# First layer's MLP in phases, with seven block products for most of its first matrix

## The chip, the core and the metric

The kernel runs on one core of a Trainium2 chip. The metric is device time in microseconds. Five engines work side by side, each through its own queue in order: TensorE (PE, matmuls, with its weight loads as PEld), VectorE (DVE), ScalarE (ACT), GpSimd (POOL) and SyncE (SP), whose queue issues nearly all the transfers.

## What is computed

A two-layer decoder trunk over 1024 tokens of width 1024. Layer 0 mixes by an mLSTM, layer 1 by latent attention. Each layer ends with the same kind of MLP:

```
h = modulate(rmsnorm(x, g2), shift, scale)
y = square(relu(h @ w1)) @ w2          # w1 1024 x 4096, w2 4096 x 1024
x = x + gate * rmsnorm(y, g3)
```

The change touches the MLP of layer 0 alone, for both halves of the tokens.

## The kernel before

**Tiles and precision.** Activations are kept feature by token: a block is 128 features by 512 tokens, that is, half of the tokens (`hfs[0]` and `hfs[1]`). Each operand of a large product is split in a high and a low part: ScalarE casts the high part, VectorE subtracts it to get the low one. A product of blocks is then three matmuls (`mm3`, lines 230 to 233): low by high, high by low, high by high, summed in one PSUM bank. Weights come as 128 x 1024 `raw` tiles by SP's queue and are split into two `ws` tiles (`wsplit`, lines 189 and 190). The pools are small and shared by the whole kernel: 24 `k` tiles and 8 `hd` tiles (each 128 x 1024), 8 `ws`, 4 `raw`, and PSUM tiles `ps` (2), `pc` (2), `pm` (2, of two banks).

**The MLP** (`mlp`, line 941) is a generator over steps of 24 matmuls. A step of the first matrix (`hidden`) makes one hidden block: eight slices of the input by three matmuls, then relu and square on ScalarE and a split into an `hd` tile. A step of the second matrix (`up_cols`, line 1027) takes a group of hidden blocks and adds their share to some of the eight output blocks: for a group of four, two output blocks a step; for a group of two, four. The first group's share is copied out of PSUM by ScalarE, every later one is added to `y` by VectorE (`accumulate`, line 198 by the profile). Weights are loaded two steps ahead. A generator hands over control after each step and, where a step has two parts, once within it (`"within"`): a first-matrix step yields twice, a second-matrix step for a group of two twice, for a group of four once.

**Streams.** The list order of TensorE's work is written by hand. `two_streams(dense, other, fill)` (line 1823) weaves an MLP (`dense`) with a serial stream (`other`). Each number that `other` yields is a demand for MLP work, and each yield of the MLP counts 0.5 against it; `"align"` runs the MLP up to the next first-matrix step, and a background stream (`fill`) gets up to four steps whenever the MLP's yield is `"hid"`. When `dense` is at its end, `other` goes on alone. `go` ties the matmuls of each step to come after the last matmul of the step before (`tc.issue_after`); within a step, and on the other engines, a compile-time scheduler orders by priority and simulated time.

**Order around the change.** After the mLSTM's output projection of the second half:
1. `f0`, the MLP of half 0, groups of four; its first 20 yields beside `p1`, which is `post` of half 1 (residual, square sums, a root, `normed`, giving the MLP's input `h2`), then the rest beside `bg_latent` (ada columns, rotary tables, latent weights).
2. `two_streams(mlp(0, hfs[1], z1, [2] * 14 + [4]), mixer1(hfs[0], z0, attention_first), bg_rest())` (line 1911): the MLP of half 1 beside layer 1's mixer of half 0. `mixer1` (line 1893) is `to_x`, `latent`, four head pairs of `attention_first`, the output projection `wout` (eight steps, woven with nothing), and `post`. A pair is `prepare_pair` (line 1372: keys, values, queries; the rotary query by lines 1123 to 1124 and 1306 to 1311) in two parts, then `attend` (line 1434): scores, softmax (lines 1335 to 1339), transposes (line 1445) and the products with the values. `post` is `residual` (lines 916 to 933), `rstd_steps` (squares at 453, sums at 457, the sum matmuls at 461, the root at 463 and 426 to 430) and `normed` (480, with the low part at 474).
3. `two_streams(mlp(1, hfs[0], ...), mixer1(hfs[1], z1, attention_second))` (line 1915), whose MLP needs what `post` made.

Of the kernel before, what the change touches and what calls it, by code (L numbers as in the profile page):

```python
# [82 lines left out]
def kernel(  # L83
# [39 lines left out]
    def k4v(dt=F32, b=512):  # L123
        return k4(dt)[:, :1024].rearrange("p (a b) -> p a b", b=b)
# [7 lines left out]
    def raw(dt=F32):  # L132
        return sb.tile([P, 1024], dt, tag="raw", bufs=RAW, name=f"raw_{next(uid)}")
# [13 lines left out]
    def ps():  # L147
        return pp.tile([P, 512], F32, tag="ps", bufs=2, name=f"ps_{next(uid)}")
# [10 lines left out]
    def scratch(shape, name):  # L159
        return dr.tile(shape, F32, tag=name, bufs=1, name=name)  # L160
# [21 lines left out]
    def paced():  # L182

        return tc.issue_after(pace[0]) if pace[0] else nullcontext()

    def wsplit(r, n):
        hi = sb.tile([P, 1024], F32R, tag="ws", bufs=WS, name=f"wh_{next(uid)}")
        lo = sb.tile([P, 1024], F32R, tag="ws", bufs=WS, name=f"wl_{next(uid)}")
        nc.scalar.copy(hi[:, :n], r[:, :n])  # L189
        i = nc.vector.tensor_sub(lo[:, :n], r[:, :n], hi[:, :n].bitcast(F32))  # L190
        if follow[0]:
            pace[0] = i.ins
        return hi, lo
# [36 lines left out]
    def mm3(o, lh, ll, rh, rl, start, stop):  # L230
        nc.tensor.matmul(o, ll, rh, start=start, stop=False)  # L231
        nc.tensor.matmul(o, lh, rl, start=False, stop=False)  # L232
        pe_last[0] = nc.tensor.matmul(o, lh, rh, start=False, stop=stop)  # L233


    nc.scalar.preload_act_table_set("natural_log_exp_and_others")
# [239 lines left out]
    def normed(h, xs_, rstd, A, sh):  # L476

        for k in range(KD):
            with paced():
                nc.vector.scalar_tensor_tensor(  # L480
                    xs_[k], xs_[k], A[:, k : k + 1], rstd, ALU.mult, ALU.mult
                )
                split_mod(h.hi[k], h.lo[k], xs_[k], sh[:, k : k + 1])
            if k % 4 == 3:
                yield 1

    def along_tokens(dst, y):
# [414 lines left out]
    def x_ahead(alloc, first=False):  # L902


        def src(half):
            t = [alloc() for _ in range(4)]
            of = xt_d[half] if first else xs[:, ts(half, H)]
            for b in range(4):
                nc.sync.dma_start(
                    t[b], of[2 * b * P : (2 * b + 2) * P].rearrange("(k p) n -> p k n", p=P)  # L910
                )
            return lambda k: t[k // 2][:, k % 2]

        return src
# [23 lines left out]
    NF = DFF // P  # L938
    AHEAD = 2

    def mlp(l, hf, y, sizes, rows=False):


        w1, w2, h = mlp_w1[l], mlp_w2[l], hf.h2
        hids = {}

        def hidden(f):
            def hid(w):
# [95 lines left out]
            return lambda: wload([(0, 0, wcols(w2, i * n * P, n * P, fs[0], G))], n * P), out  # L1044

        up = up_rows if rows else up_cols
        steps, prev, f0 = [], [], 0
        for G in sizes:
            fs = list(range(f0, f0 + G))
# [8 lines left out]
        ready = []  # L1058
        for n in range(len(steps) + AHEAD):
            if n < len(steps):  # L1060
                ready.append(steps[n][0]())
            if n >= AHEAD:
                yield from steps[n - AHEAD][1](ready.pop(0))

                yield steps[(n - AHEAD + 1) % len(steps)][1].__name__


    rope_d = scratch([2, P, S], "rope_d")
# [679 lines left out]
    A1 = gain(2, NG(0, 2), adac(0, SC2))  # L1748
    B1 = gate(3, NG(0, 3), adac(0, G2))

    def post(hf, y, B, src, A, sh):
# [5 lines left out]
        yield 0  # L1757
        hf.h2 = Split()
        yield from normed(hf.h2, y, rstd, A, sh)

# [4 lines left out]
    p0 = post(hfs[0], y0, B0, x_ahead(k4v, True), A1, adac(0, SH2))  # L1765
    so = split_o(hfs[1])
    for k, _ in enumerate(og0(hfs[1], k4v)):
        if k % 2:
# [54 lines left out]
    def two_streams(dense, other, fill=iter(()), more=4):  # L1823


        traced = nc.cur_bb.bb.instructions
        at, per = ["hid"], 0

        while True:
            n = go(other)  # L1830
            if n is end:
                break
            if n == "fill":
                per, n = more, 0
# [12 lines left out]
        drain(fill)  # L1847


    p1 = post(hfs[1], y1, B0, x_ahead(hdv, True), A1, adac(0, SH2))  # L1850
    next(p1)
    z0 = FH(claim=True)
# [36 lines left out]

    z1 = FH(claim=True)  # L1890
# [72 lines left out]
```

## Time and profile before

| | us |
|---|---|
| median of 3 runs | 2397.88 |
| lowest and highest run | 2396.58, 2399.75 |
| span of the profiled execution | 2395.7 |
| TensorE busy in it | 2364.8 |
| VectorE busy | 1550.3 |
| ScalarE busy | 1054.9 |

The page gives the profiled execution's span and no run time of its own beside it. The page is read from the top: busy shares, then the span in 40 slices with the granted clock, then the groups of instructions. A group's name is its output tile, an arrow, and its inputs. Durations of matmuls overlap, since the next starts before one ends; start times give the pace. A window row gives, for a stretch, each engine's busy time and the count of its instructions, then the granted clock, the share of the DMA engines and GB/s.

### The profile page before, as it was taken

The page shows a single profiled execution, that of the slowest core. Times are in us where ns is not written, and L with a number is a line of the kernel's source. Part 1 is how long each engine was busy: PE and PEld are TensorE (multiplying, and loading weights), DVE is VectorE, ACT ScalarE, POOL GpSimd, SP SyncE. Part 2 cuts the span into 40 slices and gives each one's busy share as a digit, 9 for nine tenths or more (in the row PEclk, how much of TensorE's full clock was granted, in tenths as well). Part 3 has the DMA queues.
Part 4 walks back from the last instruction along what each step waited for, and adds up shares of the span by engine and source line. Part 5 has one row for each costly group of instructions (what it writes and reads, how often), then busy time and mean ns, then how long its engine had stood idle before and what let it go on. Part 6 is the DMA issues. An engine that isn't in the chain of part 4 may idle for free.

```text
span 2395.7 us, 30518 instructions
## 1 busy us (share of the span) xinstructions
PE 2364.8 (99%) x11621; PEld 1945.5 (81%) x11621; DVE 1550.3 (65%) x2431; ACT 1054.9 (44%) x1712; POOL 18.3 (1%) x91
## 2 busy tenths in 40 slices
PE   7999999999999999999999999999999999999998
PEld 5888888788888887888888877888888888888886
DVE  6667866858656677877764867766566386353345
ACT  4355334655333454444444554344444353443333
POOL 1000000000000000000000000000000000000000
PEclk9999999999999999999999999999999999999999
DMA  8442654544654745545543444864424354354431
GB/s 310 148 143 81 192 178 134 165 132 150 189 171 152 243 138 179 159 160 186 168 137 114 153 162 153 260 240 133 139 97 150 105 167 128 101 189 140 144 99 62
DMA packets 377106, 374.48 MB, mean 156 GB/s; under 512 B 24355, under 2 KB 282464, under 8 KB 376960
## 3 DMA queue, kind: packets, MB, share of 16 engines
q1 hardware_dynamic: 376672, 372.44, 48.9%
q8 instruction: 91, 1.49, 0.3%
q14 instruction: 55, 0.45, 0.1%
q0 software_dynamic: 288, 0.10, 0.0%
HBM read 313.24 MB, written 59.24 MB: 155 GB/s over the span
## 4 chain that ended last, share of the span: by engine, by line
PE 91%; DVE 4%; DMA 3%; ACT 1%; issue 1%; SPq 0%; DVEq 0%; ACTq 0%
PE ps L231 17%; PE ps L232 17%; PE ps L233 17%; PE pm L231 10%; PE pm L232 10%; PE pm L233 10%; PE pc L1445 1%; PE pc L231 1%; PE pc L233 1%; PE pc L232 1%; PE pm L815 1%; PE pm L1331 1%; DMA raw<-in_mlp_w_dram 1%; DVE wl L190 1%; PE pm L1325 1%
## 5 line engine op out<-in xcount | busy, mean ns | idle before, releaser
L190 DVE TENSOR_TENSOR wl<-raw,wh 128x1024 fp32r<-128x1024 f32 (+2 forms) x366 | 438.7, 1202 | 449.5 <-ACT wh L189 442.3
L189 ACT CAST wh<-raw 128x1024 fp32r<-128x1024 f32 (+2 forms) x366 | 376.0, 1032 | 717.0 <-PE ps L231 392.2
L231 PE MATMUL ps<-k,wl 128*128 128x512 f32 x1528 | 611.0, 400 | 2.3 <-ACT k L671 1.4
L233 PE MATMUL ps<-k,wh 128*128 128x512 f32 x1528 | 601.0, 393 | 0.0
L232 PE MATMUL ps<-k,wh 128*128 128x512 f32 x1528 | 600.9, 393 | 0.0
L231 PEld LDWEIGHTS ps<-k,wl 128*128 128x128 f32 x1528 | 287.0, 188 | 69.7 <-issue 2.9
L233 PEld LDWEIGHTS ps<-k,wh 128*128 128x128 f32 x1528 | 287.0, 188 | 67.3 <-issue 0.5
L232 PEld LDWEIGHTS ps<-k,wh 128*128 128x128 f32 x1528 | 287.5, 188 | 63.6 <-issue 1.7
L198 DVE TENSOR_TENSOR k<-k,pm 128x512 f32<-128x512 f32 (+1 forms) x254 | 210.9, 859 | 107.0 <-PE pm L233 106.5
L231 PE MATMUL pm<-hd,wl 128*128 128x512 f32 x512 | 202.0, 394 | 0.4 <-ACT hd L470 0.4
L233 PE MATMUL pm<-hd,wh 128*128 128x512 f32 x512 | 199.8, 391 | 0.0
L232 PE MATMUL pm<-hd,wh 128*128 128x512 f32 x512 | 199.5, 390 | 0.2 <-DVE hd L471 0.2
L231 PE MATMUL pm<-wh,hd 128*128 128x512 f32 x488 | 192.9, 395 | 3.2 <-ACT raw L1337 2.9
L232 PE MATMUL pm<-wl,hd 128*128 128x512 f32 x488 | 191.3, 392 | 0.0
L233 PE MATMUL pm<-wh,hd 128*128 128x512 f32 x488 | 190.3, 390 | 0.0
L360 DVE SCALAR_TENSOR_TENSOR tma<-raw,cond,tma 128x512 f32<-128x512 f32 x168 | 125.6, 747 | 20.6 <-DMA raw<-in_kv_ada_w_dram 14.6
L471 DVE TENSOR_TENSOR hd<-tmp,hd 128x512 fp32r<-128x512 f32 x128 | 88.3, 690 | 56.8 <-ACT hd L470 56.5
L1337 ACT ACTIVATE raw<-pm,sm 128x128 f32<-128x128 f32 (+3 forms) x64 | 47.5, 742 | 151.3 <-DVE sm L1336 122.7
L232 PEld LDWEIGHTS pm<-hd,wh 128*128 128x128 f32 x512 | 96.2, 188 | 21.3 <-DVE hd L471 0.5
L231 PEld LDWEIGHTS pm<-hd,wl 128*128 128x128 f32 x512 | 96.1, 188 | 21.2 <-ACT hd L470 0.8
L233 PEld LDWEIGHTS pm<-hd,wh 128*128 128x128 f32 x512 | 96.1, 188 | 21.1
L231 PEld LDWEIGHTS pm<-wh,hd 128*128 128x128 f32 x488 | 91.6, 188 | 24.9 <-ACT raw L1337 5.5
(347 smaller groups left out, 3414.5 us busy)
## 6 DMA issues: line engine op xcount, KB each, us to landing
raw<-in_mlp_w_dram SPq DMA_DIRECT2D x256, 512.0 KB, 4.1
raw<-in_ada_w_dram SPq DMA_DIRECT2D x80, 512.0 KB, 4.3
raw<-in_a_w_in_dram SPq DMA_DIRECT2D x48, 512.0 KB, 4.1
xs<-k SPq DMA_DIRECT2D x40, 256.0 KB, 4.8
raw<-in_kv_ada_w_dram SPq DMA_DIRECT2D x16, 512.0 KB, 3.8
raw<-in_a_w_out_dram SPq DMA_DIRECT2D x16, 512.0 KB, 4.6
kd<-k SPq DMA_DIRECT2D x32, 256.0 KB, 3.7
vd<-k SPq DMA_DIRECT2D x32, 256.0 KB, 5.0
```

The lines of the kernel that those rows point to most:

```text
L189: nc.scalar.copy(hi[:, :n], r[:, :n])
L190: i = nc.vector.tensor_sub(lo[:, :n], r[:, :n], hi[:, :n].bitcast(F32))
L198: return f(*a, **k)
L231: nc.tensor.matmul(o, ll, rh, start=start, stop=False)
L232: nc.tensor.matmul(o, lh, rl, start=False, stop=False)
L233: pe_last[0] = nc.tensor.matmul(o, lh, rh, start=False, stop=stop)
L360: nc.vector.scalar_tensor_tensor(acc, r[:, kk], cond[:, k : k + 1], acc, ALU.mult, ALU.add)
L471: nc.vector.tensor_sub(lo, u, hi.bitcast(F32))
L815: nc.tensor.matmul(nv[:, r, i], hf.PT[p_][:, r, cs], v[:, 2 * p_ + r], start=g == 0, stop=True,)
L1325: nc.tensor.matmul(o[:, :w], ql, kh, start=True, stop=False)
L1331: nc.tensor.matmul(o[:, :w], qh, kh, start=False, stop=True)
L1337: nc.scalar.activation(pr[:, :n], f, AF.Exp, bias=m, scale=SCALE, accum_out=l)
```

## The change

The MLP of layer 0 runs in phases:
1. `up_front`: six pairs of hidden blocks (12 steps) of half 0 as before, but the result goes to the DRAM tensor `hidd`. Beside it runs `p1`, two of its steps for each step here, and now with `kept1`, which makes sums and differences of the input blocks of both halves and their splits (`b22` and parts 4 to 7); the plain blocks 0 and 1 of half 1 are saved in `b12`.
2. `seven`: the other ten pairs, for both halves at once. Hidden pair by input halves by token halves is a 2 x 2 by 2 x 2 product of blocks; it is made of seven products of four slices, with sums of weight blocks (`load`) and of results (`product`), which share PSUM banks. `both_halves` applies relu and square and stores both halves in `hidd`. Every third product gives the background a step.
3. The second matrix of half 0 (`mlp(..., stored=True)`): hidden pairs are fetched from `hidd` and split into `k` tiles, groups of four; beside it the rest of `bg_latent`.
4. The second layer-1 stream's MLP is `up_front` of half 1 (six pairs), then its stored second matrix, beside the unchanged `mixer1(hfs[0], ...)` and `bg_rest`.

The core of the diff:

```
-    def mlp(l, hf, y, sizes, rows=False):
+    hidd = scratch([2, NF // 2, P, 2 * H], "hidd")
+    def up_front(l, hf, pairs):
+            def hid(w):
+                pt = ps()
+                for k in range(KD):
+                    if k == KD // 2:
+                        yield "within"
+                    mm3(pt, w[0][:, k], w[1][:, k], h.hi[k], h.lo[k], k == 0, k == KD - 1)
+                if f % 2 == 0:
+                    at[0] = k4v()
+                s = at[0][:, f % 2]
+                with tc.high_priority(PRIO):
+                    nc.scalar.activation(s, pt, AF.Relu)
+                    nc.scalar.activation(s, s, AF.Square)
+                    if f % 2:
+                        nc.sync.dma_start(hidd[hf.i, f // 2], at[0].rearrange("p a b -> p (a b)"))
...
+    def seven(l, pairs, B, out):
+                A = wsplit(r1, 1024)
+                t1, t2 = raw(), raw()
+                nc.vector.tensor_add(t2[:, lo_], r2[:, lo_], r2[:, hi_])
+                nc.vector.tensor_sub(t1[:, hi_], t2[:, lo_], r1[:, lo_])
+                nc.vector.tensor_sub(t1[:, lo_], r1[:, lo_], r2[:, lo_])
+                nc.vector.tensor_sub(t2[:, hi_], r1[:, hi_], t1[:, hi_])
+                T1 = wsplit(t1, 1024)
...
+                T2 = wsplit(t2, 1024)
+                nc.scalar.copy(a22[:, lo_], r2[:, hi_])
+                nc.vector.tensor_sub(a22[:, hi_], r2[:, hi_], a22[:, lo_].bitcast(F32))
...
+            for u, i in ((cur, 1), (prev, 5), (cur, 2), (prev, 4), (cur, 6), (prev, 3), (cur, 7)):
+                if u:
+                    product(u, i)
+                    yield "hid"
...
+        def fetch(f):
+            with tc.high_priority(PRIO):
+                r, hi, lo = raw(), k4v(F32R), k4v(F32R)
+                nc.sync.dma_start(r, hidd[hf.i, f // 2])
+                split_wide(hi, lo, r.rearrange("p (a b) -> p a b", b=512))
...
+        if stored:
...
+            for v in ahead_of(steps):
+                n += v != "within"
+                yield v if v == "within" else ("hid", "out")[n % 2]
+            return
...
-    f0 = mlp(0, hfs[0], z0, [4] * 8)
-    for n in range(20):
-        if next(f0) != "within":
-            next(p1, None)
+    for v in up_front(0, hfs[0], range(ALONE)):
+        if v != "within":
+            next(p1, None)
+            next(p1, None)
     drain(p1)
-    two_streams(f0, behind(bg_latent(), 4))
+    bgl = bg_latent()
+    traced = nc.cur_bb.bb.instructions
+    f0, n = seven(0, range(ALONE, NF // 2), blocks, both_halves), 0
+    while go(f0) is not end:
+        pace[0] = next(i for i in reversed(traced) if i.engine == dve)
+        n += 1
+        if n % 3 == 0:
+            next(bgl, None)
...
+    two_streams(mlp(0, hfs[0], z0, [], stored=True), behind(bgl, 4))
...
-    two_streams(mlp(0, hfs[1], z1, [2] * 14 + [4]), mixer1(hfs[0], z0, attention_first), bg_rest())
+    two_streams(
+        chain(up_front(0, hfs[1], range(ALONE)), mlp(0, hfs[1], z1, [], stored=True)),
+        mixer1(hfs[0], z0, attention_first), bg_rest(),
+    )
```

`kept1`, in short: after the modulation it forms, from `y0` (half 0) and `y1` (half 1), eight wide differences on VectorE, then ten wide splits (ScalarE and VectorE).

More of the change, by code (lines that the diff above doesn't have):

```diff
@@ L939, with ahead_of, hidden @@
     AHEAD = 2
-    def mlp(l, hf, y, sizes, rows=False):
+    hidd = scratch([2, NF // 2, P, 2 * H], "hidd")
+    def ahead_of(steps):
+        ready = []
+        for n in range(len(steps) + AHEAD):
+            if n < len(steps):
+                ready.append(steps[n][0]())
+            if n >= AHEAD:
+                yield from steps[n - AHEAD][1](ready.pop(0))
+                yield steps[(n - AHEAD + 1) % len(steps)][1].__name__
+    def up_front(l, hf, pairs):
+        w1, h = mlp_w1[l], hf.h2
+        at = {}
+        def hidden(f):
+            def hid(w):
[12 more added lines that the diff above has]
+                        nc.sync.dma_start(hidd[hf.i, f // 2], at[0].rearrange("p a b -> p (a b)"))
+            return lambda: wload([(0, 0, wcols(w1, f * P))], P), hid
+        yield from ahead_of([hidden(f) for p_ in pairs for f in (2 * p_, 2 * p_ + 1)])
@@ L944, in mlp @@
+    def mlp(l, hf, y, sizes, rows=False, stored=False):
         w1, w2, h = mlp_w1[l], mlp_w2[l], hf.h2
         hids = {}
+        def fetch(f):
+            with tc.high_priority(PRIO):
+                r, hi, lo = raw(), k4v(F32R), k4v(F32R)
+                nc.sync.dma_start(r, hidd[hf.i, f // 2])
+                split_wide(hi, lo, r.rearrange("p (a b) -> p a b", b=512))
+            for e in range(2):
+                hids[f + e] = (hi[:, e], lo[:, e])
         def hidden(f):
@@ L1046, in mlp, with both @@
         up = up_rows if rows else up_cols
+        if stored:
+            fetch(0)
+            fetch(2)
+            steps = []
+            for g in range(NF // 4):
+                for i in range(4):
+                    load, run = up(list(range(4 * g, 4 * g + 4)), i, g == NF // 4 - 1)
+                    def both(load=load, f=4 * g + 2 * i):
+                        w = load()
+                        if i >= 2 and f < NF:
+                            fetch(f)
+                        return w
+                    steps.append((both, run))
+            n = 0
+            for v in ahead_of(steps):
+                n += v != "within"
+                yield v if v == "within" else ("hid", "out")[n % 2]
+            return
         steps, prev, f0 = [], [], 0
@@ L1057, in mlp @@
         steps += [up(prev, i, True) for i in range(len(prev))]
[L1058 to L1065, printed above, removed]
+        yield from ahead_of(steps)
     rope_d = scratch([2, P, S], "rope_d")
@@ L1749, with post @@
     B1 = gate(3, NG(0, 3), adac(0, G2))
[L1751 removed]
+    def post(hf, y, B, src, A, sh, kept=None):
         yield from residual(y, hf.i, B, src, (2, 2)[hf.i])
@@ L1757, in post @@
         yield 0
+        if kept:
+            yield from kept(rstd)
+            return
         hf.h2 = Split()
```

145 lines of the change are left out of this document (137 added, 8 removed).

## The prediction

> **What bounds the kernel now.** I read the page first (span, engine shares, the clock row), then the table of windows over the first layer's MLP, then the order of instructions on TensorE and VectorE there.
>
> ```profile
> span 2395.7 us, 30518 instructions
> PE 2364.8 (99%) x11621; PEld 1945.5 (81%) x11621; DVE 1550.3 (65%) x2431; ACT 1054.9 (44%) x1712; POOL 18.3 (1%) x91
> PEclk9999999999999999999999999999999999999999
> ```
>
> TensorE is occupied almost without a break and its clock is never held back for long. So a matmul taken out is worth its place in the queue, and any wait that TensorE gets anew is paid in full. These are the two sides of the sum.
>
> ```profile
> 1103.30:1175.70 72.40, 72.14 (x375) 60.27 (x374) 55.22 (x96) 30.97 (x58) 0.82 (x4) 1.00 0.54 168
> 1242.50:1303.70 61.20, 61.20 (x265) 49.68 (x264) 21.89 (x22) 22.18 (x31) 0.00 (x0) 1.00 0.31 95
> 1303.70:1343.20 39.50, 39.50 (x172) 31.94 (x171) 35.80 (x45) 19.97 (x30) 0.00 (x0) 1.00 0.62 200
> ```
>
> The columns are the stretch, its length, then busy time and count of PE, weight loads, DVE, ACT and POOL, the clock and the DMA. All three stretches lie in the second token half's MLP, which is interleaved with layer 1's attention of the first half (`mixer1`): one head pair, the output projection, and the wait between the two sums of the norm after it. TensorE is full in all of them, although the mixer's own chain is serial. What fills it is the other stream, the MLP.
>
> **What a matmul is worth.** The mean durations of the groups (about 390 ns) overlap. The queue's pace is read from start times:
>
> ```profile
> 1110.71 0.39 PE L231 MATMUL ps<-k,wl 128*128 128x512 f32 x1
> ...
> 1116.04 0.39 PE L233 MATMUL ps<-k,wh 128*128 128x512 f32 x1
> 1116.27 0.39 PE L231 MATMUL pm<-hd,wl 128*128 128x512 f32 x1
> ...
> 1121.51 0.39 PE L233 MATMUL pm<-hd,wh 128*128 128x512 f32 x1
> ...
> 1125.14 0.40 PE L231 MATMUL ps<-k,wl 128*128 128x512 f32 x1
> ...
> 1130.70 0.93 PE L1445 MATMUL pc<-ident,raw 128*128 128x128 f32 x7
> ```
>
> 24 matmuls of a first-matrix step run from 1110.71 to 1116.27: 5.56 us, 0.2317 us each. The 23 intervals of the second-matrix step after it, whose moving operand lies in hd tiles, take 5.24 us: 0.2278 each. The Trainium skill (TensorE: Matmul & The Clock Gate, Back-to-back issue gap) states about 131 ns sustained at 512 columns. By that, an estimate, the saving below would be 16 us instead of 28; the rows show 0.2317 and decide.
>
> **Part by part.**
>
> *Seven products.* For a pair of hidden blocks the plain way is 2 blocks x 8 slices x 3 matmuls x 2 halves = 96; seven products of 4 slices x 3 are 84. Ten pairs go this way (16 less the six of `ALONE`): 120 matmuls less, x 0.2317 = **-28 us**. All of it lies on the path, TensorE being full.
>
> *Second matrix from k tiles.* The hidden blocks now come back from DRAM into k tiles, where they lay in hd tiles. If the operand's place makes the 0.0039 us between the two paces, 64 steps x 24 x 0.0039 = 6 us; if not, 0. The only visible difference between the two step kinds is that place, so nearer the upper: **+4**.
>
> *Preparing the blocks (`kept1`).*
>
> ```profile
> 451.98 0.69 DVE L463 TENSOR_SCALAR tmc<-pc 128x512 f32<-128x512 f32 x1 [1.38 <-PE pc L461]
> ...
> 456.21 5.39 DVE L480 SCALAR_TENSOR_TENSOR hd<-hd,mods,tmc 128x512 f32<-128x512 f32 x8
> ...
> 509.72 4.73 DVE L927 SCALAR_TENSOR_TENSOR k<-k,mods,tmc 128x512 f32<-128x512 f32 x7
> ...
> 518.57 2.50 DVE L930 TENSOR_TENSOR k<-k,hd 128x512 f32<-128x512 f32 x4
> ...
> 525.66 2.87 DVE L457 TENSOR_TENSOR tmc<-tmc,tmc 128x512 f32<-128x512 f32 x4
> ```
>
> ```profile
> L190 DVE TENSOR_TENSOR wl<-raw,wh 128x1024 fp32r<-128x1024 f32 x350 | 426.6, 1222 | 444.5 <-ACT wh L189 440.1 <-PE ps L233 2.9 <-DMA lw<-wl 0.9
> L189 ACT CAST wh<-raw 128x1024 fp32r<-128x1024 f32 x350 | 365.3, 1048 | 708.4 <-PE ps L231 391.8 <-DMA raw<-in_mlp_w_dram 101.4 <-PE pm L231 80.4
> L470 ACT CAST hd<-tmp 128x512 fp32r<-128x512 f32 x128 | 79.5, 621 | 3.4
> ```
>
> VectorE must do, before the blocks are ready: residual 8 x 0.67 + 8 x 0.62 = 10, square sums 7 x 0.65 = 5, two roots of four narrow operations 5, modulation 8 x 0.67 = 5, ten wide splits and eight wide block differences at 1.22 = 22: 47 us. Beside it stand 12 weight splits (15) and the first two loads of `seven` with three wide and five narrow operations each (14): 76. TensorE has 12 steps x 5.56 = 67 us, and the first pair's products 1 and 2 (24 matmuls, 5.6 us) need only old blocks: 72. Late by 4, and by holes in the chain besides: **+6** (0 to 15). Queued behind VectorE's work are those weight splits, and TensorE's third product waits for it.
>
> *The seven-block phase.* 84 matmuls last 19.5 us a pair. VectorE has per pair 6.9 for the load, three PSUM sums (2), the two maxima (1.9) and two to three background steps (some 3): 14; ScalarE three wide casts and a narrow one (3.8), four narrow evacuations at 0.62 (2.5), two wide squares (2.1): 9. Neither binds. There are 8 `ws` tiles and a pair takes 7, so the next pair's first part is complete only after product 3 of the pair before, one product (12 x 0.2317 = 2.8 us) ahead of its use, for 1.05 + 1.22 of work: **+2** (0 to 10). Its PSUM reads lie three products behind the writes and cost nothing while that holds.
>
> *Through DRAM.*
>
> ```profile
> raw<-in_mlp_w_dram SPq DMA_DIRECT2D x256, 512.0 KB, 4.1
> raw<-oT SPq DMA_DIRECT2D x6, 512.0 KB, 5.0
> ```
>
> 32 stores and 32 fetches of 512 KB join SP's queue, 20 weight loads leave it. A fetch is issued two steps (11 us) or more ahead and needs a landing of 4 to 5 and a 2.3 us split: hidden, **+1** (0 to 5). VectorE loses 28 of 56 wide sums of the second half's second matrix and its narrow splits; it isn't the bound, so this gains nothing.
>
> *The cover of the attention.* This is the term that decides. `two_streams` spends the MLP stream by count of its yields: a demand of 1 by the mixer takes two yields. Before, a first-matrix step and a group-of-two second-matrix step both yield twice in 24 matmuls; the stream of the second half has 124 yields, 62 demands. The mixer asks for 7 (`to_x`) + 4 (latent) + 4 pairs x 8 + 1 + 1 + 11 (`post`) = 56. The tally agrees with the rows: between the sums at 1303.7 and 1343.2 it gives demands of 1 + 1 + 5, so 168 matmuls and four of the sums at the edges, and the row counts 172.
> Now the stream is six pairs (12 steps, 24 yields) and the stored second matrix in groups of four, whose steps have one yield in 24 matmuls: 32. That is 56 yields, 28 demands. 7 + 4 + 1 use up the first 24 yields; the 16 demands left reach through pair 0 (7) and pair 1 (8) to the first demand of pair 2. From the second part of pair 2 on nothing is left beside the mixer: two pairs, the projection and `post` run alone, where before 672 matmuls (156 us) lay between their steps. The work of TensorE is the same, done earlier and twice as dense; the waits become visible. TensorE's order is bound step to step by `go`, and the next stream's first step needs `post`'s result, so nothing later can fill in.
>
> A pair's two long chains:
>
> ```profile
> 1113.63 0.68 DVE L1123 TENSOR_TENSOR tmc<-pc,hd 128x512 f32<-128x512 f32 x1
> ...
> 1116.62 0.68 DVE L1124 TENSOR_TENSOR tmc<-tmc,tmc 128x512 f32<-128x512 f32 x1
> ...
> 1119.56 0.69 DVE L1311 TENSOR_TENSOR k<-tmc,tmp 64x512 fp32r<-64x512 f32 x1
> ...
> 1128.92 0.35 DVE L1339 TENSOR_SCALAR raw<-raw,sm 128x256 f32<-128x256 f32 x1
> ```
>
> Rotary query: L1123 0.68, then 1116.62 to 1120.25: 4.3 us from the last query matmul to the first score. Softmax: the first scores end at 1125.14 and the last probabilities at 1129.27: 4.1. Shorter waits (splits before the products, the second softmax) some 2. Floor 8.4 a pair; with a weight or a raw tile late, up to 25. I take 13, nearer the rows: two pairs **+26** (17 to 50). The projection, whose operand comes partly by DRAM: **+2** (0 to 8).
>
> `post`: evacuation, square and sum 2; root, 451.98 to 456.21, and before it two sum matmuls of under 0.4 each, 5; residual and square sums 15; root 5; modulation up to the first low part, 5.4 and one more narrow operation, 6: 33, and a foreign split between: **+34** (28 to 45).
>
> *The clock.*
>
> ```profile
> 20.00:25.00 5.00, 3.42 (x24) 2.00 (x20) 2.97 (x7) 2.58 (x3) 0.00 (x0) 0.96 1.09 356
> 25.00:30.00 5.00, 1.97 (x5) 0.48 (x5) 4.96 (x9) 2.74 (x5) 0.00 (x0) 0.50 1.05 387
> 30.00:35.00 5.00, 5.00 (x19) 3.61 (x18) 4.96 (x7) 0.76 (x1) 0.00 (x0) 0.86 1.05 385
> ```
>
> ```profile
> 28.03 0.80 PE L231 MATMUL pm<-k,wl 128*128 128x512 f32 x1 [4.36 <-ACT k L473]
> ```
>
> After one wait of 4.36 us the granted clock stood at half, and a matmul at twice its pace, until into the next 5 us: some 1 to 3 us lost. Seven such waits (two in each pair, three in `post`), nearer the lower as most are shorter: **+8** (0 to 20). The Trainium skill (TensorE: Matmul & The Clock Gate, HAM oscillation) warns of TensorE gaps over about 3.4 us, with half of such a window lost after each; by it the term would be 12 and the sum 4 higher, an estimate. The trace agrees as far as this one gap goes.
>
> *Sum.* -28 + 4 + 6 + 2 + 1 + 26 + 2 + 34 + 8 = +55. On the profiled span 2395.7 this makes 2450.7. The page gives no other time of that execution; the runs' median, 2397.88, is 2.2 above the span. So **2453 us**.
>
> **Rivals.**
> *Not slower.* The dry stretch costs next to nothing: the compile-time order finds matmuls of a neighbouring step for the gaps, since a step is tied only to the last matmul of the one before. For it: the tie is loose. Against it: `post` is one chain of 28 us at least, and nothing behind it is ready. It decides where the stretch (26 + 2 + 34 + 8 = 70 here) falls below 15; at nothing the time is 2398 - 28 + 13 = 2383.
> *Starved products.* The `ws` tiles make every pair of the seven-block phase wait a product: 10 x 2.8 = 28 in place of 2, 2479; the saving is gone, so that the change doesn't do what it says. For it: 7 of 8 tiles. Against: 2.3 us of work in 2.8.
> *Longer chains.* Raw tiles (4, held by softmax and weights) delay each lone pair to 25, `post` takes 45 and the clock 20: +24 + 11 + 12, 2500. For it: all these share four tiles. Against: without the MLP its loads are gone too.
>
> **How the numbers follow.** Forecast 0.72, starved 0.09, longer 0.09, not slower 0.10. Differences under 0.2% (4.8 us) can't be told from none here. Not slower gives faster 0.08 and same 0.02; the forecast's low tail (all low ends: -28 + 17 + 28 = +17, 2415) adds 0.01 to same; slower 0.89. The range 2420 to 2500 holds the forecast but for its low tail and both slow rivals.
>
> **What would show it.** Right: about 120 matmuls fewer (11501); TensorE full in the seven-block phase; its busy digits falling once, in the second half's MLP before the second layer-1 stream, with waits for L1311's and L1339's kind and a gap of some 30 us in `post`; the clock row below 9 there. Wrong: no such hole, or MLP matmuls still between the steps of pair 3; or waits spread over the seven products.

## The result and the profile after

The changed kernel takes 2543.97 us (median of 4 runs, 2537.52 to 2547.45) against 2398.82 for the kernel before in the same set (4 runs, 2396.58 to 2400.61): 1.060 times as long, 95% interval 1.0583 to 1.0616. The profiled execution took 2543.9 us, its span is 2542.1. The forecast was 2453 with a range to 2500: slower was right, but +145 us came where +55 was forecast. Nearly all of it arises between 440 and 1609 us of the changed kernel. The matmul that follows the first 2550 starts at 439.09 us before and at 440.38 after, and with 4400 matmuls still to come after one, 933.9 and 933.5 us of the spans remain.

From the page of the changed kernel, the lines that answer to those of before:

```profile
span 2542.1 us, 30600 instructions
PE 2385.8 (94%) x11501; PEld 1945.8 (77%) x11501; DVE 1621.5 (64%) x2501; ACT 1089.5 (43%) x1708; POOL 17.2 (1%) x83
...
PE   7999999979997999979999777999999999999998
...
PEclk9999999989998999989999888999999999999999
```

The matmul count fell by exactly the 120 of the forecast, 11621 to 11501. All the same the time rose: TensorE is now idle in many places between slices 9 and 25 (64 us each), not in one. The forecast expected one such stretch, in the second half's MLP.

The table of windows of the changed kernel, one row a stage (length, busy time and count of PE, weight loads, DVE, ACT, POOL, then granted clock, DMA share, GB/s):

```profile
527.80:544.40 16.60, 1.03 (x4) 0.20 (x2) 14.33 (x18) 11.68 (x17) 0.00 (x0) 0.62 0.33 110
585.00:770.00 185.00, 185.00 (x809) 150.58 (x808) 107.33 (x149) 73.04 (x93) 0.00 (x0) 1.00 0.46 145
791.00:991.00 200.00, 184.41 (x776) 146.87 (x775) 158.05 (x201) 81.03 (x84) 0.00 (x0) 0.97 0.78 250
1091.00:1146.00 55.00, 39.43 (x161) 30.48 (x160) 37.40 (x51) 23.91 (x31) 0.00 (x0) 0.84 0.68 226
1376.00:1458.00 82.00, 61.34 (x327) 49.85 (x325) 48.01 (x111) 31.82 (x72) 1.21 (x8) 0.89 0.32 96
1458.00:1508.00 50.00, 47.31 (x192) 37.88 (x193) 17.00 (x19) 19.29 (x27) 0.39 (x4) 0.94 0.50 140
1508.00:1546.00 38.00, 5.03 (x6) 1.43 (x7) 28.46 (x44) 17.27 (x28) 0.00 (x0) 0.50 0.52 180
```

Read from the top: one hole of 16 us while the blocks are prepared; the seven-block phase, full over 185 us; the first half's stored second matrix, which loses 15.6 of 200 us and some clock; the start of the second half's stored matrix beside the attention, with 15.6 of 55 us idle; then the lone pairs 2 and 3, the projection, and the norm's gap. The last three rows are the dry stretch of the forecast, and it starts where the tally of yields put it: the last MLP matmul beside the attention is at 1375.99, in pair 2. The seven-block phase, the second row, is full as forecast; the first, third and fourth rows hold what the forecast got wrong or left out.

From here on, line numbers are those of the changed kernel; experiments may be shifted by a few.

### The profile page after: what moved, and what is told of

It is laid out like the page before. It is cut to its first block, busy times and chain, and to the rows that moved or that the text cites. A ratio compares the mean times of both kernels' runs of the same rounds, so it can differ in the third digit from the quotient of the medians.

```text
span 2542.1 us, 30600 instructions
## 1 busy us (share of the span) xinstructions
PE 2385.8 (94%) x11501; PEld 1945.8 (77%) x11501; DVE 1621.5 (64%) x2501; ACT 1089.5 (43%) x1708; POOL 17.2 (1%) x83
## 4 chain that ended last, share of the span: by engine, by line
PE 75%; DVE 9%; DMA 9%; ACT 4%; issue 2%; SPq 0%; ACTq 0%; DVEq 0%
PE ps L232 14%; PE ps L233 14%; PE ps L234 14%; PE pm L232 7%; PE pm L233 7%; PE pm L234 7%; DMA raw<-hidd 3%; DMA raw<-in_mlp_w_dram 3%; DVE wl L190 2%; DVE k L490 1%; ACT wh L189 1%; PE pc L1613 1%; DVE tma L361 1%; ACT k L489 1%; PE pc L233 1%
## 5 line engine op out<-in xcount | busy, mean ns | idle before, releaser
L190 DVE TENSOR_TENSOR wl<-raw,wh 128x1024 fp32r<-128x1024 f32 (+1 forms) x356 | 426.9, 1201 | 433.3 <-ACT wh L189 395.4
L189 ACT CAST wh<-raw 128x1024 fp32r<-128x1024 f32 (+1 forms) x356 | 365.6, 1031 | 674.9 <-PE ps L232 350.8
L232 PE MATMUL ps<-k,wl 128*128 128x512 f32 x1328 | 534.0, 402 | 30.8 <-ACT k L989 17.6
L234 PE MATMUL ps<-k,wh 128*128 128x512 f32 x1328 | 524.2, 395 | 0.0
L233 PE MATMUL ps<-k,wh 128*128 128x512 f32 x1308 | 518.3, 396 | 4.3 <-DVE k L475 4.3
L232 PE MATMUL pm<-k,wl 128*128 128x512 f32 x636 | 259.7, 408 | 42.0 <-DVE wl L190 15.6
L234 PEld LDWEIGHTS ps<-k,wh 128*128 128x128 f32 x1328 | 251.2, 189 | 58.9 <-issue 0.5
L233 PEld LDWEIGHTS ps<-k,wh 128*128 128x128 f32 x1308 | 247.9, 190 | 60.1 <-DVE k L475 4.9
L233 PE MATMUL pm<-k,wh 128*128 128x512 f32 x636 | 256.4, 403 | 5.9 <-DVE k L490 5.9
L234 PE MATMUL pm<-k,wh 128*128 128x512 f32 x636 | 255.7, 402 | 0.0
L232 PEld LDWEIGHTS pm<-k,wl 128*128 128x128 f32 x636 | 123.3, 194 | 75.6 <-ACT k L489 16.6
L233 PEld LDWEIGHTS pm<-k,wh 128*128 128x128 f32 x636 | 123.2, 194 | 39.0 <-DVE k L490 9.1
L234 PEld LDWEIGHTS pm<-k,wh 128*128 128x128 f32 x636 | 122.8, 193 | 28.5
L489 ACT CAST k<-raw 128x1024 fp32r<-128x1024 f32 x66 | 68.9, 1049 | 100.4 <-DMA raw<-hidd 95.7
L232 PEld LDWEIGHTS pm<-wh,hd 128*128 128x128 f32 x488 | 91.6, 188 | 23.9 <-ACT raw L1505 4.5
L234 PEld LDWEIGHTS pm<-wh,hd 128*128 128x128 f32 x488 | 91.6, 188 | 20.2 <-issue 0.5
```

Of the source, the lines that this page charges most:

```text
L232: nc.tensor.matmul(o, ll, rh, start=start, stop=False, **m)
L233: nc.tensor.matmul(o, lh, rl, start=False, stop=False, **m)
L489: nc.scalar.copy(hi, u)
```

## The experiments

Times are medians of 4 runs of each kernel, 7 of the kernel before; "after" is 2543.97.

**1. The dry stretch by itself, on the kernel before.**

```diff
-    two_streams(mlp(0, hfs[1], z1, [2] * 14 + [4]), mixer1(...), bg_rest())
+    two_streams((v for v in mlp(0, hfs[1], z1, [2] * 14 + [4]) if v != "within"), mixer1(...), bg_rest())
```

> The kernel before, with the second half's MLP yielding once a step in place of twice: 62 yields, 31 demands, of the 56 that the attention asks for. Nothing is stored, no products are saved, the tiles are as before. It is the dry stretch alone, starting at about the first demands of pair 2. Theory: two lone pairs with some 11 us of gaps each, the projection 5, the norm 31 to 39, the clock 10 to 15: 60 to 85 us more than 2398, 2458 to 2483, with a gap of about 20 us or more before the second sum of the norm. Rival (the loss of the changed kernel in this stretch comes from its stored blocks and tiles, not from the missing cover): under 30 us more, below 2428.

Measured: 2473.71 us (2468.22 to 2475.36) against 2398.30, +75.4; ratio 1.0307 (1.0287 to 1.0327). The order of TensorE's matmuls that waited, at the norm of this kernel (start, duration, then in brackets the idle time and what ended it):

```profile
1436.96 2.02 PE L461 MATMUL pc<-tmc,ones 128*128 128x512 f32 x2 [2.63 <-DVE tmc L457]
1460.72 2.04 PE L461 MATMUL pc<-tmc,ones 128*128 128x512 f32 x2 [21.73 <-DVE tmc L457]
1469.54 0.80 PE L231 MATMUL ps<-k,wl 128*128 128x512 f32 x1 [6.78 <-ACT k L473]
1474.68 0.80 PE L232 MATMUL ps<-k,wh 128*128 128x512 f32 x1 [4.35 <-DVE k L474]
```

The changed kernel has the same four, with nearly the same numbers:

```profile
1508.03 2.02 PE L462 MATMUL pc<-tmc,ones 128*128 128x512 f32 x2 [2.64 <-DVE tmc L458]
1531.86 2.05 PE L462 MATMUL pc<-tmc,ones 128*128 128x512 f32 x2 [21.81 <-DVE tmc L458]
1540.69 0.80 PE L232 MATMUL ps<-k,wl 128*128 128x512 f32 x1 [6.78 <-ACT k L474]
1545.83 0.80 PE L233 MATMUL ps<-k,wh 128*128 128x512 f32 x1 [4.35 <-DVE k L475]
```

The theory holds. Nothing here is stored or multiplied differently; only the MLP's yields run out early, and that alone costs 75 us. (Some 6 us of TensorE's waits in this run stand before the dry stretch, such as one of 2.98 us at 1018.42 at the attention's first splits, where the MLP's work is spent twice as fast.)

**2. Giving the cover back.** The stored steps of the second half yield three times.

```diff
                     for q, f in enumerate(fs):
                         c_ = ts(m - i * n, P)
+                        if stored and hf.i and (m % 2, q) in ((0, 3), (1, 2)):
+                            yield "within"
```

> The stored second matrix of the second half yields three times per step of 24 matmuls (after 9, 6 and 9) in place of once; nothing else of the changed kernel is touched. By the tally its stream then has 24 + 96 yields, 60 demands, against the 56 that the attention asks for, so the MLP reaches to the end of the norm behind the projection. Theory (the dry stretch is the largest loss): the lone pairs 2 and 3 (each about 41 us with some 11 us of gaps), the projection (5) and the norm (31 of waits in one place, 39 with the slow first block behind it), with the low clock between, lose their waits: 65 to 85 us less than 2544, so 2460 to 2480, and no gap over 8 us between the two sums of the norm. Rival (thin cover): 18.9 matmuls per demand in place of 24 leave part of every wait of the four pairs open, and the norm's demands get only 16 matmuls each: 10 to 35 us less, 2510 to 2535.

Measured: 2515.73 us (2513.59 to 2519.48), 28 less than after; ratio to before 1.0488 (1.0468 to 1.0508). That is the rival's range. By the edit the three parts of a step are 9, 9 and 6 matmuls, not 9, 6 and 9. The norm's long gap is gone (the largest wait left in it is 6.4 us), but a new wait appeared in each pair, here in the order of TensorE's matmuls:

```profile
1307.19 0.69 PE L1495 MATMUL pm<-k,k 128*128 128x384 f32 x1 [3.69 <-ACT raw L1507]
...
1382.67 0.69 PE L1495 MATMUL pm<-k,k 128*128 128x384 f32 x1 [4.65 <-ACT raw L1507]
```

L1495 is a score, L1507 the exponential of the softmax before: the score's two-bank PSUM tile (`pm`) is free only when the exponential has read it. So moving cover does not return what the lone stretch cost. With three yields a step, a demand gets 16 matmuls of a stored step where each took 24 before: less cover has to hide the same chains. This run does not tell the thin cover and the shared tile apart; experiment 3 changes the tile (and the adds that read it).

**3. PSUM.** As 2, with the sums of the stored steps in one-bank tiles.

```diff
-                    pt = b2[:, m % 2]
+                    if stored and hf.i:
+                        pt = ps()
...
+                    if stored and hf.i:
+                        accumulate(m, y[m], pt)
```

> As a1_thirds, and the stored second matrix of the second half sums each block of 12 matmuls in a one-bank ps tile of its own, where a step of 24 held a two-bank pm tile. In a1_thirds eight waits on pm tiles that the scores or the MLP had to share until the softmax's exponential (1.5 to 5.1 us each, 29 us together, the four of 4.2 to 5.1 at the first scores of a round) took the place of the dry stretch. Theory (two pm tiles are too few when every MLP step holds one for 5.6 us; before, every second step was a first-matrix step in a ps tile): these waits go: 20 to 32 us less than 2516, so 2484 to 2496. Rival (the scores would wait for the softmax of the round before in any order, or the ps tiles, two as well, become the new place of the wait): within 8 of 2516.

Measured: 2503.36 us (2498.99 to 2505.74), 12.4 less than 2. Between the two expectations. The waits on `pm` tiles that the softmax holds, 25.5 us of idle time together in the trace of 2, are all gone, but waits on `ps` tiles stand in their place (2.7, 2.3, 3.7, 3.3 us and smaller, ended by the copy of the attention's output or by the splits of keys and queries). The shared PSUM tiles were a cause of their own, about half of it mended here.

**4. Tiles for the blocks computed ahead.**

```diff
-                if f % 2 == 0:
-                    at[0] = k4v()
-                s = at[0][:, f % 2]
+                s = tmp()
...
+                    nc.sync.dma_start(hidd[hf.i, f // 2][:, ts(f % 2, 512)], s)
```

> The first-matrix results of the six pairs computed ahead go through the tmp tiles (one block each, stored as 256 KB) in place of halves of a k tile. Theory (k tiles are short while the block differences are made, and the relu waits for one): the gap of 16 us before the first-matrix step that followed the second sum goes, with the cold clock behind it: 16 to 22 us less than 2544, so 2522 to 2528. Rival (VectorE is late with the differences, as the prediction put it, and the k tile is only where that shows): the wait returns at the third product of the seven-block phase or at its weights: within 5 us of 2544.

Measured: 2529.73 us (2522.87 to 2532.58), 14.2 less than after; ratio to before 1.0541 (1.0517 to 1.0564). Both sides were partly right. ScalarE's order in the changed kernel, at the hole of 16 us:

```profile
539.36 1.03 ACT L489 CAST k<-k 128x1024 fp32r<-128x1024 f32 x1
...
542.80 1.04 ACT L489 CAST hd<-hd 128x1024 fp32r<-128x1024 f32 x1
543.75 1.06 ACT L989 ACTIVATE k<-ps 128x512 f32<-128x512 f32 x2
```

TensorE's order, there and in the experiment:

```profile
544.39 0.79 PE L232 MATMUL ps<-k,wl 128*128 128x512 f32 x1 [15.57 <-ACT k L989]
```

```profile
573.07 0.80 PE L233 MATMUL ps<-hd,wh 128*128 128x512 f32 x1 [6.28 <-DVE hd L490]
```

L989 is the relu that empties the PSUM tile of a first-matrix block. It stands in ScalarE's queue behind the modulation and the wide splits of the other half's blocks, and runs twice in a row at 543.75, for two products, the later of which started its last matmul at 527.56; with another tile to write to, relus ran at 526.06, 532.77, 538.00 and 544.24, one a product. So the k tile put it there. With that gone, VectorE's lateness shows: 6.3 us at the first product that needs a new block, which is the wait the forecast had priced.

**5. The way back from DRAM.** All but the first two fetches of each half are left out; the stores stay, and the stored matrix uses the first four blocks for all.

```diff
         def fetch(f):
+            if f >= 4:
+                for e in range(2):
+                    hids[f + e] = hids[f + e - 4]
+                return
```

> The stored second matrix of both halves fetches only the first four hidden blocks from DRAM and uses them for all 32: 28 of 32 fetches, with their raw tiles, landings and splits, are left out (the stores stay). Theory (the fetches take raw tiles and split time that the weights of the stored steps need): most of the waits in the first half's stored matrix (about 25 us after the start) and of those on splits in the second go: 20 to 35 us less than 2544, so 2509 to 2524. Rival (those waits belong to the latent weights prepared beside the stored matrix, which hold raw and weight tiles themselves): 0 to 8 us less, 2536 to 2544.

Measured: 2515.36 us (2513.51 to 2519.63), 28.6 less than after; ratio 1.0487 (1.0464 to 1.0510). The theory holds. Its window over the first half's stored matrix, against 184.41 of 200 above:

```profile
791.00:1004.00 213.00, 211.79 (x920) 170.51 (x918) 150.10 (x204) 70.96 (x84) 0.00 (x0) 1.00 0.60 194
```

The latent weights are prepared beside it as before, yet TensorE is full and the clock whole. In the changed kernel most of the waits there, 11.2 us in four, end with `wl L190`, a weight split:

```profile
935.22 0.77 PE L232 MATMUL pm<-k,wl 128*128 128x512 f32 x1 [3.77 <-DVE wl L190]
949.80 0.47 PE L232 MATMUL pm<-k,wl 128*128 128x512 f32 x1 [1.80 <-DVE wl L190]
965.85 0.77 PE L232 MATMUL pm<-k,wl 128*128 128x512 f32 x1 [4.57 <-DVE wl L190]
```

So there the fetches delay the weights rather than wait themselves. Of the gain, 22 us had come by the first relu wait of the second half's blocks (1004.79 in place of 1027.23). The starts of both stored matrices keep their waits.

**6. The same transfers without raw tiles.**

```diff
-                r, hi, lo = raw(), k4v(F32R), k4v(F32R)
-                nc.sync.dma_start(r, hidd[hf.i, f // 2])
+                hi, lo = k4v(F32R), k4v(F32R)
+                r = lo.bitcast(F32)
+                nc.sync.dma_start(r.rearrange("p a b -> p (a b)"), hidd[hf.i, f // 2])
```

> As the changed kernel, but the fetch of a stored pair lands in the k tile that later holds its low part and is split in place, so that it takes no raw tile; the transfer, its size and its split remain. Theory (the four raw tiles are what the fetches and the stored steps' weights compete for; leaving the fetches out gave 29 us): 12 to 26 us less than 2544, 2518 to 2532. Rival (the landings of 4.4 us and the splits on ScalarE and VectorE are the price, whatever tile they use): within 6 of 2544.

Measured: 2553.24 us (2552.16 to 2555.86), 9.3 more than after; ratio 1.0645 (1.0629 to 1.0660). Neither expectation. The trace divides it: the first relu wait of the second half's blocks stands at 1016.68 in place of 1027.2, so the first half gained 10.5 us, as raw tiles would have it; but the second half's stored matrix starts with one wait of 16.9 us, and SP issues the first six fetches only from 1115.46 (the first two at 1102.25 and 1113.39 in the changed kernel). A fetch now needs its k tile from the start of the transfer, which is the likely reason; SP shows no wait of its own just before them. That start only takes back what the first half gained. Part of the rest shows in the four waits on `pm` tiles beside the attention: 10.2 us together in the changed kernel, where they are listed further down, and 4.5, 6.4, 5.3 and 3.8, 20 us, here. Why they grew was not tested.

```profile
1125.73 0.80 PE L232 MATMUL pm<-k,wl 128*128 128x512 f32 x1 [16.88 <-ACT k L489]
```

**7. Two attempts at the starts.** The blocks' read-back moved from ahead of the first half's stored matrix to behind 24 of its 32 steps; and hd tiles for the second half's first two fetches.

```diff
-    again = [[k4v(F32R), k4v(F32R)] for _ in range(2)]
...
+        for n, v in enumerate(g):
+            if n == 24:
+                again = [[k4v(F32R), k4v(F32R)] for _ in range(2)]
```

> As the changed kernel, but the two stored k pairs of the second half's normed input (b12) are read back and split after 24 of the 32 steps of the first half's stored matrix, where the changed kernel does it ahead of them: four k tiles, two raw tiles and two splits less at the start of the stored matrix. Theory (that start, with 10 us of waits between 776 and 790 and 5 between 811 and 818, is short of k tiles, since the block parts hold nine until the last products and the read-back takes four): 8 to 15 us less than 2544, 2529 to 2536. Rival (the waits are the landings and the splits of the first fetches, which wait for the last blocks in any case): within 5 of 2544.

```diff
-                r, hi, lo = raw(), k4v(F32R), k4v(F32R)
+                new = hdv if hf.i and f < 4 else k4v
+                r, hi, lo = raw(), new(F32R), new(F32R)
```

> As the changed kernel, but the first two fetched pairs of the second half lie in hd tiles in place of k tiles (four hd tiles for one group). Fetching in place had made this start dearer (17 us of wait in one place where the changed kernel has 7.5, 3.6 and 1.2), so k tiles, of which the mixer's normed input and the MLP's input hold eight each there, are suspected. Theory (k tiles): most of the 12 us of waits at the start of the second half's stored matrix go, with the clock behind it 8 to 15 us less than 2544, 2529 to 2536. Rival (the raw tiles and the order of SP's queue, behind the attention's own stores, set when the fetch lands): within 5 of 2544.

Measured: 2544.41 us (2540.11 to 2551.56) and 2539.22 (2538.24 to 2545.39): +0.4 and -4.8. The rival in both: k tiles do not set these starts. What the changed kernel's queues show at the second one, SP first, then ScalarE, then TensorE:

```profile
1102.25 1.15 SPq L1097 DMA_DIRECT2D raw<-hidd  x1
...
1115.95 0.52 SPq L211 DMA_DIRECT2D raw<-in_mlp_w_dram  x1
```

```profile
1121.62 1.04 ACT L189 CAST wh<-raw 128x1024 fp32r<-128x1024 f32 x1 [2.50 <-DMA raw<-in_mlp_w_dram]
```

```profile
1126.07 0.79 PE L232 MATMUL pm<-k,wl 128*128 128x512 f32 x1 [7.11 <-ACT k L489]
1129.67 0.79 PE L233 MATMUL pm<-k,wh 128*128 128x512 f32 x1 [2.80 <-DVE k L490]
```

The fetch is issued at 1102.25, 24 us ahead of its use; its split (L489) stands in ScalarE's queue behind the cast of a weight tile whose transfer SP issued only at 1115.95. With hd tiles the order of these is the same. So the early fetch helps nothing. The waits of SP's own queue show what holds the weight up, from 1104 to 1112.5 (what waited, for what, total, times, longest):

```profile
SPq L992 <- ACT k L990: 7.2, 1, 7.2
```

SP stands for 7.2 us at the store of the last pair computed ahead (`L992`), until its square (`L990`) is done at 1112.3; the second fetch and the weight are issued behind it. The weight's own split ends only at 1123.9, some 5 of the 7.1 us into TensorE's wait; the rest is the fetch's split behind it. So the order of two queues, SP's and ScalarE's, makes the wait in this trace. No run moved that store, so what it is worth stays open.

**8. Is the saving real?** Product 2 computed twice in every pair, 120 matmuls more.

```diff
-            for k in range(4):
+            for k in range(4) if i != 2 else (0, 1, 2, 3, 0, 1, 2, 3):
```

> As the changed kernel, but product 2 of every pair of the seven-block phase is computed twice (the second time over the first), so that TensorE has 96 matmuls a pair again while all loads, splits, sums and tiles stay those of seven: 120 matmuls more. Theory (the phase is bound by TensorE's own pace and the 28 us saved are real, hidden in the sum under larger losses): 25 to 29 us more than 2544, 2569 to 2573. Rival (the phase waits for weights or splits, so that a product less saves little): under 12 us more.

Measured: 2568.51 us (2565.68 to 2569.42), 24.5 more than after; ratio 1.0704 (1.0687 to 1.0722). Just under the band of 25 to 29, twice the rival's bound. The phase runs at TensorE's own pace, and the products saved are worth what the queue's pace says, within the 10 us by which runs of after differ.

**9. The mendings together.**

> a4_ps, a5_inplace and a2_tmp together. If the losses add as the single runs gave them: 2544 - 28 (thirds) - 26 (ps) - 14 (tmp) - 19 (fetch in place) = 2457, 2440 to 2475. Rival (the waits are links of the same chains, so that one mended shows the next): 2480 to 2500. Below 2398 would say that the phases cost nothing once the tiles are right; by the theory they still cost the block preparation (7), the starts of the stored matrix (15) and a thinner cover (20 and more).

> All mendings together, each where the single runs had it help: three yields a stored step in the second half, its sums in ps tiles in every second step and in pm in the others, tmp tiles for the blocks computed ahead, the fetch in place for the first half alone, the late read-back. If they add: 2488 (the earlier sum of mendings) less 8 (late read-back), less 9 (the start of the second half's stored matrix, 17 with the fetch in place, 8 without), less 5 to 10 (ps and pm in turn): 2460 to 2470. Rival (each mended wait shows the next one in the same chains): 2480 to 2495.

> As d3_best, with ps tiles in all stored steps of the second half. Theory (waits of TensorE for one-bank tiles held by the value and query blocks of the attention, 2 to 4 us each in a4_ps, are the price of leaving pm altogether): 5 to 15 us more than d3_best. Rival (pm held for a whole step of 24 matmuls is dearer): less than d3_best.

> As d4_best2 (2474), with the first two fetched pairs of the second half in hd tiles. Theory: 8 to 14 us less, 2460 to 2466. Rival: within 5 of 2474.

Measured, in this order: 2488.41 us (2486.53 to 2489.94), 2484.82 (2484.05 to 2487.96), 2473.70 (2472.66 to 2481.11) and 2474.67 (2474.29 to 2478.62). The first missed its sum (2457) by 31 us and the second the middle of its own (2465) by 20: the gains of single mendings do not add. The third, expected 5 to 15 above the second, came out 11 below it: leaving `pm` altogether is better than taking turns. The hd tiles give nothing here (the rival, within 5 of 2474). The best is 70 us better than after and still 1.0319 (1.0302 to 1.0335) times before. Its windows, from the first half's stored matrix to the norm:

```profile
762.00:965.00 203.00, 186.17 (x785) 149.30 (x786) 169.06 (x220) 86.09 (x89) 0.00 (x0) 0.97 0.78 267
965.00:1065.00 100.00, 100.00 (x429) 79.92 (x428) 65.53 (x89) 47.47 (x73) 0.00 (x0) 1.00 0.59 186
1065.00:1364.00 299.00, 264.48 (x1319) 214.18 (x1318) 224.51 (x397) 126.88 (x218) 3.40 (x18) 0.95 0.60 194
1364.00:1480.00 116.00, 101.19 (x415) 79.94 (x414) 73.17 (x97) 49.83 (x68) 0.59 (x6) 0.93 0.54 171
```

The idle time is now spread: 17, 0, 35 and 15 us, and the clock is below 1 in three of the four. No version here beats the kernel before.

## Why the prediction was right in direction and wrong in size

*The saving, -28: right.* 120 matmuls fewer, about 24.5 us by experiment 8.

*Second matrix from k tiles, +4: right.* From 938.21 to 947.49, 40 intervals of a stored step's matmuls are 0.232 us each, as in a first-matrix step, against 0.2278 from hd tiles: some 6 us over the 64 steps.

*The seven-block phase, +2: right.* TensorE is busy 185.00 of 185 us in it. The rival of starved products is out.

*The cover of the attention, 26 + 2 + 34, and the clock, 8: right in place, and together 70 against 75.4 measured alone* (experiment 1), *but the sum came out in part by luck.* In the changed kernel the lone pairs idle 20.7 us in 82 (forecast 26, with some loss of clock), the projection 2.7 (2), the norm 2.64 + 21.81 + 6.78 + 4.35 = 35.6 (34). The tally of yields found the place. So the rival that the stretch costs nothing is out, and the rival of longer chains too: the chains were not longer. But the pages of experiment 1 and of the kernel before split the price otherwise than the forecast. TensorE idles 57.6 us more (2473.6 less 2385.1, against 2395.7 less 2364.8): 14.5 in the lone pairs (forecast 26), 1.3 at the projection, 35.5 at the norm, and some 6 earlier, which no term held. And its busy time is 20.3 us longer for the same 11621 matmuls: they ran slower, at a mean granted clock of 0.984 against 0.997. So the clock's price is up to 20 us, where 8 was forecast. A term too high and a term too low nearly cancel.

*Preparing the blocks (`kept1`), +6: wrong by a term left out.* VectorE's lateness was 6.3 us in experiment 4, as worked out. But the step counted only VectorE's work and not the tiles: the relu of the blocks computed ahead got its k tile late, for 16 us. Experiment 4 gives 14 us for that, net of the lateness that then shows.

*Through DRAM, "hidden, +1": the step that failed most plainly.* It argued from lead time (11 us) against landing plus split (4 to 5, plus 2.3), the first rule one reaches for. Leaving the fetches out gave 28.6 us. A fetch also takes a raw tile and places in two queues from the weights of the same steps; experiment 6 shows some 10 us of it as raw tiles in the first half. Which part of the rest is queue and which is tile is not settled.

*What no term held.* The changed kernel's waits that stayed when the fetches were left out: the starts of the two stored matrices, some 9 and 10 us; two waits of 4.4 and 0.8 at the attention's first splits (at 1098); and, with the MLP still beside the attention, four on `pm` tiles, 10.2 us here and 7.8 without the fetches:

```profile
1159.95 0.80 PE L232 MATMUL pm<-k,wl 128*128 128x512 f32 x1 [2.66 <-ACT raw L1505]
1192.70 0.51 PE L232 MATMUL pm<-k,wl 128*128 128x512 f32 x1 [2.78 <-ACT raw L1505]
...
1289.18 0.49 PE L232 MATMUL pm<-k,wl 128*128 128x512 f32 x1 [2.92 <-ACT raw L1505]
...
1320.93 0.50 PE L232 MATMUL pm<-k,wl 128*128 128x512 f32 x1 [1.88 <-ACT raw L1505]
```

Before, every second step of the MLP was a first-matrix step, which sums in `ps`. The change puts all of those first, so that beside the scores stand only steps that hold a `pm` tile for 24 matmuls, and the scores need both. The forecast asked when the cover ends but not which PSUM tiles the cover uses while it lasts.

As a sum: -24.5 (experiment 8) + 75.4 (1) + 14.2 + 6.3 (4) + 28.6 (5) = 100 of the 145; the starts, the four `pm` waits and the waits at the first splits, as they stand without the fetches, are 19 + 8 + 5 = 32 more, read from the trace and not each tested. The remaining 13 us are not assigned, nor are overlaps between the terms: the 75.4 already holds a wait of 2.98 us at the first splits.

*The clock, once more.* The two pages divide the 146.4 us of span without any experiment. TensorE idles 125.4 us more than before (2542.1 less 2385.8, against 2395.7 less 2364.8), and its busy time is 21.0 us longer although 120 matmuls, 24.5 us, are gone. So the others took some 45 us longer, at a mean granted clock of 0.971 against 0.997, and most of that is the low clock's. The forecast priced the clock at 8 because it counted seven waits; TensorE's order in the changed kernel has 31 of over 1 us from the block preparation to the norm.

*The range.* It was built from the bounds of the terms that were seen. Three shortages of the same kind (k, raw and PSUM tiles) were each held at nearly nothing; one of them was named in a rival for the lone pairs only, where it did not occur.

## What to carry to other kernels

Where one engine is full, price a reordering by what it takes from the cover of the other stream, in yields and demands; here that tally gave the place, and a sum within 10% in which two errors nearly cancelled. Then go through every pool (SBUF tags, landing tiles, PSUM banks) and count the tiles that live together at the new place: a transfer issued early is not hidden if it holds a tile, or a place in a queue, that the bound engine's next operand needs. And do not count on cover being given back by spreading it thinner: with 16 matmuls a demand in place of 24 there was a wait in every pair again, part of it for PSUM tiles.

## What the runs showed of the hardware

The clock falls after shorter waits than the forecast's single row of 4.36 us suggested. At the projection of the changed kernel, TensorE started its last matmul before the wait at 1455.10 and the next at 1458.08, an interval of 2.98 us; the order of its matmuls after it:

```profile
1458.67 0.63 PE L233 MATMUL ps<-k,wh 128*128 128x512 f32 x1
1459.10 0.63 PE L234 MATMUL ps<-k,wh 128*128 128x512 f32 x1
1459.52 0.63 PE L232 MATMUL ps<-k,wl 128*128 128x512 f32 x1
1459.95 0.63 PE L233 MATMUL ps<-k,wh 128*128 128x512 f32 x1
```

```profile
1458.00:1463.00 5.00, 4.92 (x12) 3.86 (x13) 3.60 (x5) 2.93 (x4) 0.00 (x0) 0.50 1.21 290
1463.00:1468.00 5.00, 5.00 (x22) 4.05 (x21) 1.30 (x2) 1.92 (x3) 0.00 (x0) 0.93 1.09 261
```

Starts are 0.43 us apart in place of 0.2317 until 1463.36, twelve matmuls, so 2.5 us are lost on top of the wait; after the wait of 15.57 us at 544.39 it was ten or eleven matmuls, some 2 us, and after one of 3.77 us at 935.22 six or seven, some 1.4 us. So the price did not grow with the wait.

Waits that stand alone show where it begins. Two of the `pm` waits listed above, each with no other wait of over 0.5 us in the 25 us before it, are those of 2.66 us at 1159.95 and 2.78 at 1192.70: each was followed by seven or eight matmuls about 0.43 us apart. After those of 1.88 us (1320.93) and 1.80 (949.80) none was. The windows with the waits of 2.78 and 1.88:

```profile
1190.00:1200.00 10.00, 7.30 (x25) 5.83 (x26) 7.68 (x18) 4.11 (x8) 0.00 (x0) 0.83 0.37 121
1317.00:1327.00 10.00, 8.12 (x37) 6.22 (x36) 7.68 (x22) 4.75 (x10) 0.00 (x0) 1.00 0.22 64
```

By these rows several waits of some 2.7 us cost more of the clock than one long one. The Trainium skill (TensorE: Matmul & The Clock Gate, HAM oscillation) gives gaps over about 3.4 us as the ones to avoid. By its trace this kernel pays for 2.66 as well. The interval of 2.98 followed another of 1.62 us within 5 us, and the trace does not tell their shares apart. The forecast took from that section that half of such a window is lost at each gap and made 12 us of it; the kernel measured there was throttled for about 1.67 us at each gap and lost half of that, by which seven waits make about 6 us, an estimate. Experiment 1 measured up to 20.
